# Hymba layer step on one core: first norm about a pivot, four x loads, and a different order of the first loads and products

## The chip, the cores and the metric

One NeuronCore of a Trainium2 chip runs the whole program in one launch. The metric is the device time in microseconds (us); lower is better. The kernel before took 1599.39 us as the median of three runs (1597.56 to 1601.09).

## What is computed

The reference is one layer of a hybrid recurrent transformer, for 256 prompt tokens and 8 x 4 sample tokens (288 tokens, 2048 features, float32). Only its beginning matters here:

```
mod = jax.nn.silu(c) @ w_ada + b_ada
sh1, sc1, g1, sh2, sc2, g2 = jnp.split(mod[:, None, :], 6, axis=-1)
h = layer_norm(x) * (1 + sc1) + sh1
z = (h @ w_in).astype(f32)
```

`layer_norm` takes mean and variance over the 2048 features of each token. After `z` come two recurrent mixers, an output projection, a second norm, a convolutional feed-forward part and a third norm. The rest of the program is the same text in both kernels.

## The kernel before

**Layout.** Features lie on the 128 partitions, tokens on the free axis: x is 16 tiles `xs[k]` of 128x288. A sum over features is a matmul by a matrix of ones: `colsum` adds a tile into one of four groups of 32 rows of a PSUM bank, and `total` copies that bank on ACT and multiplies it by ones again, so that every partition holds the sum.

**Products.** Weights come in granules of 128x1024 float32 (512 KB): `load_to` issues the load into a `raw` buffer on the SP queue, `high_to` casts it to float32r on ACT (`whi`), `low_to` subtracts on DVE (`wlo`). An activation tile is split the same way (`split`). `products` issues, per 128x128 block, three matmuls: whi by the high part, whi by the low part, wlo by the high part. `granule` keeps a few granules ahead. `raw` and `wlo` share seven buffers (NR), `whi` has four (NH).

**adaLN.** `mod` is made in steps of one 512 KB load (`araw`, NA = 7 buffers) and a group of small float32 matmuls each (`ada_step`). UNITS_ADA says which columns a unit of steps gives: ADA_K = (2, 2, 2, 2, 4, 4) means that the first unit gives shift and scale for two tiles of x, after eight steps. When a unit is done, `ada_finish` transposes the sums on DVE, adds the bias (`pks`), and puts `hidden(k)` on a list of background work; `tick` advances that list. `hidden` makes tile k of h.

**The start** (function `start`). SP issues ct, 16 loads of x, seven adaLN loads, two constants (`cs`, `pks`), and then what the steps and granules ask for. PE sums the 16 tiles; DVE scales to the mean `mu`; then each tile is centred (two in three on DVE, one in three on POOL), squared (ACT or DVE) and summed; `rstd_of` makes 1/sqrt(var) with Ln and Exp on ACT and three DVE operations. Then w_in is multiplied in five groups of k-tiles, KG = (2, 2, 4, 4, 4), for the first 28 (NSPLIT) column tiles: group 0 takes seven granules of four column tiles each, so it can begin when two tiles of h are there. Partial sums are copied out of PSUM by ACT in group 0 and added by DVE in later groups (`partial`). After every granule `credit` grows, and when it reaches four, four adaLN steps follow.

**What sets the order.** The schedule is the order in which the program text is written, engine by engine; each engine works its queue in order, and SP issues DMAs in order, waiting at each for its buffer to be free.

## Time and profile before

| | us |
|---|---|
| median of three runs | 1599.39 |
| the profiled execution | 1595.16 |
| its span, first to last instruction | 1593.4 |
| PE busy | 1552.8 (97%) |
| DVE busy | 1029.1 (65%) |
| ACT busy | 697.0 (44%) |
| POOL busy | 278.1 (17%) |

The profiled execution is 1.8 us longer than its span and 4.2 us shorter than the median. A busy share is an average over the span; the rows further below take stretches of it. PE is TensorE's matmuls, PEld its weight loads, DVE is VectorE, ACT ScalarE, POOL GpSimd, and SPq the queue on which SyncE issues DMAs. A float32 matmul leaves two records in the trace, a float32r one a single record.

### The profile page before, as it was taken

The numbers are of one execution on the slowest core, as the hardware profiler recorded it, in microseconds if no ns is written. First come the engines' busy times: TensorE is split into PE (matmuls) and PEld (weight loads), VectorE is DVE, ScalarE is ACT, GpSimd is POOL, SyncE is SP. The second block draws the span as 40 slices with busy tenths as digits, with TensorE's granted clock in tenths as the row PEclk, the third lists the DMA queues.
The fourth block names the chain that finished last, engine by engine and source line by source line (L and its number), as shares of the span: only waits on it lengthen the run. The fifth ranks groups of instructions, "written<-read, shape, count | busy, mean of one in ns | idle before, by whom it ended". The sixth has DMA issues, their size and how long they took to land.

```text
span 1593.4 us, 31779 instructions
## 1 busy us (share of the span) xinstructions
PE 1552.8 (97%) x12607; PEld 1454.4 (91%) x12607; DVE 1029.1 (65%) x2074; ACT 697.0 (44%) x1224; POOL 278.1 (17%) x434
## 2 busy tenths in 40 slices
PE   6999999999999989998999999999999999999998
PEld 3999989788898878886999999999999999999997
DVE  4566667887888778778855554555555555555555
ACT  3522335556656555335644333334343334343343
POOL 1000011444354343225311100011110001111000
PEclk9999999999999999998999999999999999999999
DMA  9898855778868778783544555555555555554552
GB/s 338 325 344 318 313 197 156 279 255 296 305 227 314 266 270 313 258 308 105 169 160 164 168 162 163 169 168 163 168 164 158 163 178 162 169 164 164 167 153 72
DMA packets 99269, 340.79 MB, mean 214 GB/s; under 512 B 11433, under 2 KB 18097, under 8 KB 98097
## 3 DMA queue, kind: packets, MB, share of 16 engines
q1 hardware_dynamic: 96624, 328.55, 60.1%
q0 software_dynamic: 2496, 10.22, 1.6%
q8 instruction: 99, 1.62, 0.4%
q14 instruction: 50, 0.40, 0.1%
HBM read 326.51 MB, written 12.21 MB: 213 GB/s over the span
## 4 chain that ended last, share of the span: by engine, by line
PE 84%; DVE 9%; ACT 3%; DMA 2%; issue 1%; SPq 0%; POOL 0%; ACTq 0%; DVEq 0%
PE mm L169 69%; PE sd L169 11%; DVE t L156 4%; PE ad L169 3%; ACT t L166 1%; DVE wlo L156 1%; DVE t L159 1%; DVE t L163 1%; ACT whi L229 1%; DMA raw<-w_in_b 1%; DVE c L159 1%; DMA t<-xt 1%; DMA raw<-w_out_b 0%; DMA pks<-pk 0%; ACT t L189 0%
## 5 line engine op out<-in xcount | busy, mean ns | idle before, releaser
L169 PE MATMUL mm<-t,whi 128*128 128x288 f32 (+1 forms) x4624 | 937.7, 298 | 16.9 <-ACT whi L229 9.2
L169 PEld LDWEIGHTS mm<-t,whi 128*128 128x128 f32 (+1 forms) x4624 | 741.4, 188 | 31.1 <-ACT whi L229 10.5
L169 PE MATMUL mm<-t,wlo 128*128 128x288 f32 x2312 | 683.4, 296 | 5.0 <-DVE wlo L156 5.0
L229 ACT CAST whi<-raw 128x1024 fp32r<-128x1024 f32 (+2 forms) x413 | 423.1, 1027 | 449.8 <-PE mm L169 226.0
L156 DVE TENSOR_TENSOR wlo<-raw,whi 128x1024 fp32r<-128x1024 f32 (+2 forms) x413 | 501.6, 1216 | 22.3 <-ACT whi L229 17.4
L169 PEld LDWEIGHTS mm<-t,wlo 128*128 128x128 f32 x2312 | 434.9, 188 | 6.8 <-DVE wlo L156 6.8
L169 PE MATMUL mm<-ff,whi 128*128 128x288 f32 x1376 | 276.1, 296 | 0.0
L169 PEld LDWEIGHTS mm<-ff,whi 128*128 128x128 f32 x1376 | 220.8, 188 | 2.5 <-issue 1.9
L166 ACT ACTIVATE t<-t 128x288 f32<-128x288 f32 (+4 forms) x329 | 126.2, 397 | 191.8 <-DVE t L156 137.6
L169 PE MATMUL mm<-ff,wlo 128*128 128x288 f32 x688 | 203.1, 295 | 0.0
L156 POOL TENSOR_TENSOR t<-t,t 128x288 f32<-128x288 f32 (+3 forms) x141 | 125.1, 896 | 183.5 <-ACT t L166 102.0
L159 DVE SCALAR_TENSOR_TENSOR t<-mm,mod,t 128x256 f32<-128x256 f32 x96 | 46.3, 482 | 149.2 <-PE mm L169 141.0
L169 PEld LDWEIGHTS mm<-ff,wlo 128*128 128x128 f32 x688 | 129.1, 188 | 0.0
L156 DVE TENSOR_TENSOR t<-t,t 128x288 f32<-128x288 f32 (+5 forms) x230 | 103.8, 473 | 24.8 <-ACT t L189 20.6
L1509 POOL COPY convo<-ext 128x2 f32<-128x2 f32 x43 | 8.0, 185 | 630.1 <-ACT ext L1503 630.1
L1504 DVE COPY ext<-mm 128x32 f32<-128x32 f32 x42 | 8.1, 192 | 141.1 <-ACT ext L1503 140.5
L169 PE MATMUL sd<-t,whi 128*128 128x288 f32 x464 | 95.5, 298 | 0.0
L169 PE MATMUL ad<-araw,csp 128*32 128x256 f32 (+1 forms) x1312 | 75.8, 362 | 0.8 <-DMA araw<-w_ada 0.8
L169 PEld LDWEIGHTS sd<-t,whi 128*128 128x128 f32 x464 | 75.9, 192 | 0.0
L156 DVE TENSOR_TENSOR t<-cv,mm 128x256 f32<-128x256 f32 x80 | 20.7, 300 | 78.9 <-PE mm L169 78.9
L169 PE MATMUL sd<-t,wlo 128*128 128x288 f32 x232 | 69.2, 298 | 0.0
L156 DVE TENSOR_TENSOR t<-t,mm 128x288 f32<-128x288 f32 x70 | 31.4, 450 | 52.6 <-PE mm L169 52.4
(253 smaller groups left out, 1171.0 us busy)
## 6 DMA issues: line engine op xcount, KB each, us to landing
araw<-w_ada SPq DMA_DIRECT2D x180, 512.0 KB, 5.6
raw<-w_up_b SPq DMA_DIRECT2D x160, 512.0 KB, 3.6
raw<-w_in_a SPq DMA_DIRECT2D x56, 512.0 KB, 6.7
raw<-w_in_b SPq DMA_DIRECT2D x56, 512.0 KB, 6.8
raw<-w_down SPq DMA_DIRECT2D x48, 512.0 KB, 3.5
raw<-w_down SPq DMA_DIRECT2D x32, 384.0 KB, 3.1
raw<-w_out_a SPq DMA_DIRECT2D x16, 512.0 KB, 6.5
raw<-w_out_b SPq DMA_DIRECT2D x16, 512.0 KB, 6.2
```

The source lines that it names most:

```text
L156: (eng or self.nc.vector).tensor_tensor(out=out, in0=a, in1=b, op=op)
L159: self.nc.vector.scalar_tensor_tensor(out=out, in0=a, scalar=s, in1=b, op0=op0, op1=op1)
L163: (eng or self.nc.vector).tensor_scalar(out=out, in0=a, scalar1=s1, scalar2=s2, op0=op0, **kw)
L166: self.nc.scalar.activation(out, a, f, **kw)
L169: self.nc.tensor.matmul(out, lhsT, rhs, start=start, stop=stop, **kw)
L229: self.nc.scalar.copy(hi[:, :w], raw[:, :w])
L1504: nc.vector.tensor_copy(se[:, :, 2:6], self.smp(pa))
L1509: nc.gpsimd.tensor_copy(co[:, j, 0:2], ext[:, TP:TP + 2])
```

## The change

All of it lies before the mixers, in about the first eighth of the program.

1. x comes in four loads of four tiles into one buffer of a pool of its own (`xin`), in place of 16 loads of one tile.
2. The norm is taken about a pivot: the mean of the first four tiles alone (`piv`). All 16 tiles have piv subtracted on DVE and are squared on ACT; one pass sums both x - piv (`s1`) and its square (`s2`). Mean offset `d` = s1/D, variance = s2/D - d*d + EPS. No tile is centred on POOL any more.
3. `normal(k)` subtracts d and multiplies by 1/std, for two tiles right away and for tile done + 2 after each granule; `hidden` loses its multiplication.
4. ADA_K begins with (1, 1, ...): the first unit gives one tile after four steps, the second the next tile after four more.
5. The order of the first loads on SP is written out, with the number of adaLN loads limited by `ad_limit` (8, 12, 15) and no longer by the number of steps done.
6. Six adaLN steps, in place of two, stand between the norm and the first granule, and the first weight cast stands after the fourth of them; five matmuls whose result nobody reads (`warm`) follow.
7. The first granule goes through `by_pass`: for all four column tiles first whi by tile 0's parts, then whi by tile 1's parts, and wlo at the very end.

The diff, cut at the places marked:

```diff
-ADA_K = (2, 2, 2, 2, 4, 4)
+ADA_K = (1, 1, 2, 2, 2, 4, 4)
...
-            if not ahead and s >= (self.ad_n if s < AD0 else max(self.ad_n, AD0 + NPRE)) + NA:
+            if s >= AD0 + NPRE and s >= max(self.ad_n, AD0 + NPRE) + NA:
                 break
...
-        xs = self.xs = [self.t288() for _ in range(KT)]
-        for k in range(KT):
-            nc.sync.dma_start(xs[k], i["xt"][:, k, :])
-        self.ada_load(NA)
+        xt = xin.tile([P, KT, T], F32, name="x")
+        for k in range(0, KT, 4):
+            nc.sync.dma_start(xt[:, k:k + 4, :], i["xt"][:, k:k + 4, :])
+        xs = self.xs = [xt[:, k, :] for k in range(KT)]
         a, b = CC["cap"][0], PK["b_ada"][1]
+        self.ad_limit = 8
+        self.ada_load(8)
+        nc.sync.dma_start(self.pks[:, :b], i["pk"][:, :b])
+        self.load_to(2)
+        self.ad_limit = 12
+        self.ada_load(12)
+        self.load_to(4)
+        self.ad_limit = 15
+        self.ada_load(15)
         nc.sync.dma_start(self.cs[:, :a], i["cst"][:, :a])
-        nc.sync.dma_start(self.pks[:, :b], i["pk"][:, :b])
...
-        sm = self.ps(T)
-        for k in range(KT):
-            self.colsum(sm, xs[k], k, KT)
-        mu = self.t288()
-        self.tsc(mu, self.total(sm), 1.0 / (32 * D), None, ALU.mult)
-        self.ada_step()
-        self.ada_step()
-        sq = self.ps(T)
-        for k in range(KT):
-            self.tt(xs[k], xs[k], mu, ALU.subtract, eng=nc.gpsimd if k % 3 == 2 else None)
-            s = self.t288()
-            if k % 4 == 3:
-                self.tt(s, xs[k], xs[k], ALU.mult)
-            else:
+        pv = self.ps(T)
+        for k in range(4):
+            self.colsum(pv, xs[k], k, 4)
+        piv = self.t288()
+        nc.scalar.mul(piv, self.total(pv), 1.0 / (32 * 4 * P))
+        s1, s2 = self.ps(T), self.ps(T)
+        for c in range(0, KT, 4):
+            sq = []
+            for k in range(c, c + 4):
+                self.tt(xs[k], xs[k], piv, ALU.subtract)
+                s = self.t288()
                 self.act(s, xs[k], AF.Square)
-            self.colsum(sq, s, k, KT)
-            if k % 4 == 1:
+                sq.append(s)
+            for k in range(c, c + 4):
+                self.colsum(s1, xs[k], k, KT)
+            for k in range(c, c + 4):
+                self.colsum(s2, sq[k - c], k, KT)
+            if c >= 8:
                 self.ada_step()
         var = self.t288()
-        self.tsc(var, self.total(sq), 1.0 / (32 * D), EPS, ALU.mult, ALU.add)
+        d = self.d = self.t288()
+        self.tsc(d, self.total(s1), 1.0 / (32 * D), None, ALU.mult)
+        self.tt(var, d, d, ALU.mult)
+        self.tsc(var, var, -EPS, None, ALU.add)
+        t2 = self.total(s2)
+        self.stt(var, t2, 1.0 / (32 * D), var, ALU.mult, ALU.subtract)
         self.rx = self.rstd_of(var)
+        for k in range(2):
+            self.normal(k)
...
-        self.load_to(2)
-        for _ in range(2):
+        for n in range(6):
+            self.ada_step()
             self.tick()
-            self.ada_step()
+            if n == 3:
+                self.tick()
+                self.high_to(1)
+        self.ad_limit = AD0
+        warm = self.ps(T)
+        for n in range(5):
+            self.mm(warm, self.ones, xs[KT - 1 - n], n == 0, n == 4)
...
+                sums = [self.ps(T, "sd" if j % 2 else "mm") for j in range(nj)] if done == 0 else None
+                if sums:
+                    self.by_pass(sums, hl, ks)
...
+                if done + 2 < KT:
+                    self.normal(done + 2)
...
+    def normal(self, k):
+        x = self.xs[k]
+        self.tt(x, x, self.d, ALU.subtract)
+        self.tt(x, x, self.rx, ALU.mult)
+
     def hidden(self, k):
...
-        self.tt(x, x, self.rx, ALU.mult)
```

**How the change moves the work.** In the rows below a name's number only tells one buffer of a kind from another.

The SP queue from the first load on, before: x tile by tile, seven adaLN loads, the constants, five more adaLN loads, then the first two weight granules (`raw`).

```order
L439 DMA t_78<-ct 128x144
L442 DMA t_80<-xt 128x288
...
L306 DMA araw_124<-w_ada 128x1024
L445 DMA cs<-cst 128x168
L446 DMA pks<-pk 128x96
L306 DMA araw_168<-w_ada 128x1024
...
L220 DMA raw_324<-w_in_a 128x1024
L220 DMA raw_326<-w_in_a 128x1024
L306 DMA araw_328<-w_ada 128x1024
L306 DMA araw_338<-w_ada 128x1024
L220 DMA raw_378<-w_in_a 128x1024
```

The same queue, changed:

```order
L441 DMA t_81<-ct 128x144
L444 DMA x<-xt 128x1152 x4
L306 DMA araw_88<-w_ada 128x1024
...
L306 DMA araw_102<-w_ada 128x1024
L449 DMA pks<-pk 128x96
L220 DMA raw_105<-w_in_a 128x1024
L220 DMA raw_107<-w_in_a 128x1024
L306 DMA araw_109<-w_ada 128x1024
...
L306 DMA araw_115<-w_ada 128x1024
L220 DMA raw_117<-w_in_a 128x1024
```

The first granule is now the ninth 512 KB load and no longer the thirteenth; the third granule (raw_117, raw_378 before) is the fifteenth and no longer the seventeenth, and `cs` goes behind all of these.

PE at the first granule, before: per column tile all six products, wlo from the third on (t_362 and t_363 are the parts of tile 0 of h, t_366 and t_367 those of tile 1).

```order
L169 MATMUL ad_159<-araw_168,csp 32x128 x8
L169 MATMUL mm_386<-t_362,whi_370 128x288
L169 MATMUL mm_386<-t_363,whi_370 128x288
L169 MATMUL mm_386<-t_362,wlo_372 128x288
L169 MATMUL mm_386<-t_366,whi_370 128x288
L169 MATMUL mm_386<-t_367,whi_370 128x288
L169 MATMUL mm_386<-t_366,wlo_372 128x288
L169 MATMUL sd_393<-t_362,whi_370 128x288
```

The same place, changed (t_388 and t_389 are tile 0, t_440 and t_441 tile 1):

```order
L169 MATMUL sd_351<-araw_102,csp 32x64 x16
L169 MATMUL sd_430<-x,ones 128x288 x5
L169 MATMUL mm_454<-t_388,whi_392 128x288
L169 MATMUL mm_454<-t_389,whi_392 128x288
L169 MATMUL sd_455<-t_388,whi_392 128x288
...
L169 MATMUL mm_454<-t_440,whi_392 128x288
L169 MATMUL mm_454<-t_441,whi_392 128x288
...
L169 MATMUL mm_454<-t_388,wlo_444 128x288
L169 MATMUL mm_454<-t_440,wlo_444 128x288
```

Eight products now need neither wlo nor tile 1, and eight more need no wlo; an adaLN step is 16 matmuls of 64 columns in the first two units, and eight of 128 before.

DVE from the third granule's low part on, before: low parts alone, and `hidden` with its multiplication (t_80 there is x).

```order
L156 TENSOR_TENSOR t_80<-t_80,t_289 128x288
L163 TENSOR_SCALAR t_352<-t_80,mod 128x256
...
L156 TENSOR_TENSOR wlo_372<-raw_324,whi_370 128x1024
L156 TENSOR_TENSOR wlo_376<-raw_326,whi_374 128x1024
L156 TENSOR_TENSOR wlo_417<-raw_378,whi_380 128x1024
L156 TENSOR_TENSOR wlo_496<-raw_382,whi_419 128x1024
```

DVE there, changed (t_263 is d, t_276 is 1/std):

```order
L156 TENSOR_TENSOR wlo_444<-raw_105,whi_392 128x1024
L156 TENSOR_TENSOR wlo_448<-raw_107,whi_446 128x1024
L156 TENSOR_TENSOR x<-x,t_263 128x288
L156 TENSOR_TENSOR x<-x,t_276 128x288
L156 TENSOR_TENSOR wlo_487<-raw_117,whi_450 128x1024
L156 TENSOR_TENSOR x<-x,t_263 128x288
L156 TENSOR_TENSOR x<-x,t_276 128x288
L156 TENSOR_TENSOR wlo_566<-raw_119,whi_489 128x1024
```

From the third granule on, the two operations of `normal` stand ahead of each granule's low part.

## Rows read from the trace of the kernel before

**Rows 1.** The page: busy time of each engine over the span.
```profile
PE 1552.8 (97%) x12607; PEld 1454.4 (91%) x12607; DVE 1029.1 (65%) x2074; ACT 697.0 (44%) x1224; POOL 278.1 (17%) x434
```

**Rows 2.** The two longest sums of PE's waits, 33 to 215 us: total, times, longest.
```profile
PE mm L169 <- ACT whi L229: 6.2, 1, 6.2
PE mm L169 <- DVE wlo L156: 2.3, 4, 1.5
```

**Rows 3.** Timeline to the first square: start, length, what, idle time before it and releaser.
```profile
3.84 7.93 PE L169 MATMUL sd<-t,ones 128*32 128x288 f32 x28 [3.84 <-DMA t<-xt]
...
12.69 0.14 PEld L169 LDWEIGHTS sd<-t,ones 128*32 128x32 f32 x2 [0.49 <-DMA t<-xt]
13.40 0.40 ACT L395 COPY t<-sd 128x288 f32<-128x288 f32 x1 [8.97 <-PE sd L169]
...
13.85 0.75 PE L169 MATMUL sd<-t,ones 128*128 128x288 f32 x2 [0.49 <-ACT t L395]
...
15.14 2.40 DVE L156 TENSOR_TENSOR t<-t,t 128x288 f32<-128x288 f32 x3
```

**Rows 4.** Timeline of DVE, ACT and PE from the last squares to the first products.
```profile
22.32 1.19 DVE L156 TENSOR_TENSOR t<-t,t 128x288 f32<-128x288 f32 x3
22.81 1.14 ACT L166 ACTIVATE t<-t 128x288 f32<-128x288 f32 x3 [0.29 <-DVE t L156]
26.29 1.08 PE L169 MATMUL ad<-araw,csp 128*32 128x128 f32 x32
26.40 0.46 DVE L163 TENSOR_SCALAR t<-sd 128x288 f32<-128x288 f32 x1 [2.40 <-PE sd L169]
26.89 0.92 ACT L166 ACTIVATE t<-t 128x288 f32<-128x288 f32 x2 [1.34 <-DVE t L163]
28.33 0.95 DVE L159 SCALAR_TENSOR_TENSOR t<-t,t 128x288 f32<-128x288 f32 x2
29.20 0.31 DVE L345 STREAM_TRANSPOSE adsb<-ad 128x128 f32<-128x128 f32 x1
30.98 0.43 ACT L189 CAST t<-t 128x288 fp32r<-128x288 f32 x1 [3.17 <-DVE t L156]
32.46 1.99 ACT L229 CAST whi<-raw 128x1024 fp32r<-128x1024 f32 x2
33.55 0.85 PE L169 MATMUL mm<-t,whi 128*128 128x288 f32 x2 [6.18 <-ACT whi L229]
```

**Rows 5.** The first two granules and the steps behind them; the third granule's cast.
```profile
34.81 0.61 PE L169 MATMUL mm<-t,wlo 128*128 128x288 f32 x1 [0.41 <-DVE wlo L156]
36.90 1.05 ACT L229 CAST whi<-raw 128x1024 fp32r<-128x1024 f32 x1 [2.46 <-DMA raw<-w_in_a]
42.96 1.95 PE L169 MATMUL sd<-araw,csp 128*32 128x128 f32 x64
44.84 0.53 PE L169 MATMUL mm<-t,whi 128*128 128x288 f32 x2
```

**Rows 6.** Stretches: us, busy time of PE, PEld, DVE, ACT, POOL, granted clock, DMA share, GB/s.
```profile
34.00:36.00 2.00, 1.59 (x7) 1.25 (x7) 1.89 (x2) 0.45 (x1) 0.00 (x0) 0.50 1.04 414
3.00:8.00 5.00, 4.16 (x12) 1.09 (x12) 0.62 (x2) 0.99 (x4) 0.00 (x0) 1.00 0.93 259
40.00:44.00 4.00, 4.00 (x63) 3.84 (x66) 1.57 (x2) 3.12 (x7) 0.00 (x0) 1.00 0.07 28
60.00:100.00 40.00, 39.77 (x509) 36.99 (x502) 29.04 (x65) 13.73 (x19) 0.00 (x0) 1.00 0.98 364
```

**Rows 7.** DMA packets from 3 to 12.5 us, and from 15 to 34 us.
```profile
DMA packets 2273, 2.64 MB, mean 278 GB/s; under 512 B 253, under 2 KB 2167, under 8 KB 2273
...
DMA packets 2374, 7.75 MB, mean 408 GB/s; under 512 B 391, under 2 KB 519, under 8 KB 2373
```

**Rows 8.** Tile vm: duration ns min/median/max, first and last start.
```profile
L169 PE MATMUL sd<-vm,stk x32: 390/400/507, 267.1 to 631.0; 96*128 96x512 f32 x32
L156 POOL TENSOR_TENSOR vm<-stk,cs x16: 1890/1894/2866, 251.2 to 620.0; 96x1024 fp32r<-96x1024 f32 x16
```

More of the change, by code (lines that the diff above doesn't have):

```diff
@@ L430, in run, with start @@
         self.ad_stop, self.ad_limit, self.ad_tag = AD0 - 4, AD0, "sd"
-        self.start()
+        with tc.tile_pool(name="xin", bufs=1) as xin:
+            self.start(xin)
         self.mixer()
         self.tail()
-    def start(self):
+    def start(self, xin):
         nc, i = self.nc, self.i
@@ L488, in start @@
                 hl = self.granule()
+                sums = [self.ps(T, "sd" if j % 2 else "mm") for j in range(nj)] if done == 0 else None
+                if sums:
+                    self.by_pass(sums, hl, ks)
                 for j in range(nj):
-                    ps = self.ps(T, "sd" if j % 2 else "mm")
-                    self.products(ps, hl, j * ks * P, self.h[k0:k0 + ks], True, True)
+                    if sums:
+                        ps = sums[j]
+                    else:
+                        ps = self.ps(T, "sd" if j % 2 else "mm")
+                        self.products(ps, hl, j * ks * P, self.h[k0:k0 + ks], True, True)
                     self.tick()
                     self.bg.append(self.partial(self.z[nj * p + j], ps, g == 0))
+                if done + 2 < KT:
+                    self.normal(done + 2)
                 self.credit += 2 if done < 14 or done % 3 == 0 else 1
@@ L499, in start, with by_pass @@
             self.tick()
+    def by_pass(self, sums, hl, ks):
+        hi, lo = hl
+        for q, (xh, xl) in enumerate(self.h[:ks]):
+            for j, ps in enumerate(sums):
+                c = slice((j * ks + q) * P, (j * ks + q + 1) * P)
+                self.mm(ps, hi[:, c], xh, q == 0, False)
+                self.mm(ps, hi[:, c], xl, False, False)
+        for j, ps in enumerate(sums):
+            for q, (xh, xl) in enumerate(self.h[:ks]):
+                c = slice((j * ks + q) * P, (j * ks + q + 1) * P)
+                self.mm(ps, lo[:, c], xh, False, q == ks - 1)
     def partial(self, a, ps, first):
```

## The prediction

> **What bounds the kernel now.** Start with the page: PE is busy for 97% of the span [rows 1]. That is an average, so look next at PE's waits, by stretch. From 33 to 215 us PE waits 6.2 us once, for the cast of its first weights, and 2.3 us in four pieces for low parts [rows 2]; between 60 and 100 us it is busy for 39.77 of 40 us [rows 6]. So from its first product on PE is the bound, and a time saved ahead of that product, or in the half-clock stretch behind it, moves the rest of the program forward, as long as PE's data keep up. The timeline says what comes ahead. The first product starts at 33.55 us [rows 4]; before it lie the arrival of x (to 12.7 us), the mean (first tile centred at 15.14) [rows 3], centring and squares (to 23.95), variance and 1/std (to 29.2), two tiles of h and the first cast [rows 4]. [...] PE's last work before was an adaLN step that ended at 27.37, 6.18 us before the first product [rows 4].
>
> All differences below are against the profiled execution (span 1593.4 us, 1.8 us around it, 1595.16 in all); the median is 4.2 us above that, and I add those at the end.
>
> **x.** Up to 12.5 us nearly all packets are under 2 KB (2167 of 2273, 1.2 KB each on average) and 278 GB/s flow; from 15 us on, with 512 KB loads, it is 408 GB/s at 3.3 KB [rows 7], and in the former stretch the engines are just as busy (share 0.93 at 259 GB/s) [rows 6]. So the size of the packets costs, and four tiles in one load give rows four times as long. I take 408 GB/s. Bounds: 278 and 408. The first tile was there at 3.84 us [rows 3]; three more (0.44 MB, 1.1 us) complete the first load at 4.9 us, and the other 12 tiles (1.77 MB, 4.3 us) end at 9.25, 3.4 us earlier than now. [...]
>
> **The norm.** The pivot needs only the first load. Four column sums (1.2 us: the last one of now takes 0.7 from its weight load at 12.69 to the copy at 13.40, and four of them overlap in part), copy 0.40, total 0.75 [rows 3], the scaling on ACT 0.40 as that copy: 4.9 + 2.75 + 0.15 of handovers = 7.85 us, where now it is 15.14. Centring is 16 DVE operations of 0.40 (1.19 for three) with the square 0.38 behind each on ACT [rows 4]: 14.25, last square 14.7, its sum 15.1. Now this takes until 23.95, because POOL shares it and three DVE operations cost 2.40 us [rows 3]. Then the price of the single pass: an adaLN step stands on PE ahead of the totals. A step is 16 records now, and two in a row take 1.08 us [rows 4], 0.54 each; in the change it is 32 records of half the columns, between 0.54 (columns count) and 1.08 us (records count). [...] Total 0.75, d, its square, -EPS and the variance on DVE 4 x 0.47 = 1.9, Ln and Exp 0.92, three DVE operations 1.45 [rows 4]: 21.05. Two `normal` 4 x 0.43 = 1.7: 22.75. From the transpose at 29.20 to the cast at 30.98 it is 1.78 with one multiplication of 0.47 [rows 4], without it 1.3: 24.05. Cast of tile 0 0.43, of the weights 1.0: **first product at 25.6 us**, 7.95 earlier.
>
> Are its weights there? Load pieces of 512 KB take 1.285 us each at 408 GB/s. The first granule is the ninth: 9.25 + 9 x 1.285 + 0.1 for pks = 20.9 us. The eighth adaLN load must wait until step 0 frees a buffer, at about 13.5 us; at that time seven pieces are queued to 18.2, so SP's wait leaves no hole. adaLN step 7 needs the eighth piece (19.6) and ends by 20.5 to 22 us; the five idle matmuls (2 records each, 0.5 us per pair) end at 23 to 24.5, ahead of the first product. They cost nothing, since PE has nothing else then.
>
> **The first two granules.** Two granules take PE 6.35 us at full clock; now they took from 33.55 to the steps at 42.96 [rows 4, 5], 9.4 us: 0.41 waiting for the low part [rows 5] and about 2.6 at half clock [rows 6]. In the change PE idles 1 to 2.5 us before the first product, against the 6.18 us after which the clock was low, so I take full clock: -2.6. `by_pass` takes the low part's wait away, but a new wait comes: eight products of tile 0 are done in 1.05 us, and tile 1 comes later. DVE makes the low part of tile 0, transposes, and makes tile 1 (1.8 us after the first product's start with its cast), then the first low part (1.15): granule 0 ends 4.1 us after its start, 29.7. Granule 1 needs a PSUM bank, the bank a copy on ACT, and that copy stands in ACT's queue behind the cast of the third granule, which is piece 15: 9.25 + 19.3 + 0.1 = 28.65, cast 1.05, copy 0.40: **30.1**. So this wait, not the low part, starts granule 1. It ends at 33.3, the four steps behind (1.95) at 35.3. In the trace of before that point is 44.84 [rows 5]: **-9.5 us**.
>
> **Behind it.** PE's order is the same from here, but for which PSUM bank a unit of adaLN uses. Do loads keep up? At 35.3 about 20 pieces are there, one fewer than at 44.84 now, for now DMA lay idle at 40 to 44 us (share 0.07) with full buffers [rows 6]; PE asks six pieces in 8.45 us, DMA can give them in 7.7. I charge 0.5 us for pauses in that stream (0 to 3). DVE gets `normal` 14 times behind granules, 0.9 us each (12.6), and loses 14 multiplications of 0.45 in `hidden` (6.3). At 60 to 100 us it is busy 29.04 of 40 [rows 6]; with nine `normal` more and four multiplications less, 35.3 of 40: it fits, tightly where a unit's two tiles of `hidden` fall together with partial sums. I charge 0.5 us (0 to 3). POOL's set-up instruction for its first two-input operation moves from before 15 us to ahead of the first `vm` at 251.2; that result lies ready at 254.1, and PE takes the first at 267.1 [rows 8]. No row shows how long the set-up takes; up to the cover of 13 us it costs nothing, and I take nothing.
>
> **Sum:** -9.5 + 0.5 + 0.5 = -8.5. Profile 1586.7; median 1599.4 - 8.5 = **1591 us**. Either bound of the uncertain terms gives 1586 at best (pauses and DVE nothing, granule 1 at 29.7, 1.8 us of scatter between runs); its own range is 1587 to 1595.
>
> **Rivals.**
> *Half clock again* (0.13). PE's work in the norm is short sums with gaps, and if the clock is low when products begin, the 2.6 us are lost again, and up to 2 more while sums run slowly: 1594 to 1596. For it: low clock after 27.37 [rows 4, 6]. Against: less idle time, the five idle matmuls.
> *x no faster* (0.07). x ends at 12.7 as now; the third granule comes 3.4 us later (at 32.1; now its cast waits for it until 36.90 [rows 5]), granule 1 at 33.5: 1594. [...] Against: packets and shares [rows 6, 7].
> *DMA is the bound from there* (0.10). At 60 to 100 us DMA is busy 0.98 at 364 GB/s [rows 6], and PE asks 372. If that is its limit, PE, started early, runs into its loads, and what stays is what the loads gained, 0 to 3.4 us: 1596 to 1599, no change or little. Against: no wait of PE for a load there [rows 2], and 408 GB/s earlier [rows 7].
> *DVE decides* (0.05), on the other side. `normal` stands ahead of each low part. If DVE has no room per granule, each of 14 granules waits 0.9 us: +12.6 against -9.5, 1602.5. It decides once DVE's work per granule passes PE's: four partial sums, one low part and one `normal`, 4 x 0.45 + 1.2 + 0.9 = 3.9 us, against 4.2 of PE. That is near, but partial sums on DVE begin only with the eighth granule, so the likely price is 3 us, 1594.
> *Forecast* (0.62); something unseen, 0.03.
>
> **The numbers.** A measurement can tell about 0.2%, 3.2 us. Faster by more: most of the forecast, half clock and slow x, a third of the DMA case: 0.82. Within: 0.13. Slower: 0.05. The range, 1586 to 1597, reaches into the DMA case.
>
> **What would show it.** Last column sum of the first load near 6 us, first centring near 8, first product near 26 us; granted clock 1.00 from there; PE's wait before granule 1 ended by ACT behind a DMA; the first four full steps done near 35 us; the waits of PE from there to 205 us still near zero. A half-clock stretch after 25 us, PE waiting for `raw` or `araw` at 40 to 100, or for wlo in the second group of granules would prove one of the rivals.

## The result, and the profile after

| | before | after |
|---|---|---|
| median, four runs of each on one chip (us) | 1600.24 | 1587.06 |
| lowest to highest | 1597.56 to 1601.87 | 1584.66 to 1588.47 |
| ratio, 95% interval | | 0.9927 [0.9914, 0.9941] |
| profiled execution | 1595.16 | 1587.27 |
| its span | 1593.4 | 1585.4 |

The changed kernel is 0.7% faster, 9 to 14 us by the interval of the ratio (the medians alone differ by 13.2). The two profiled executions differ by 8.0 us only in their spans, since that of before was one of the quicker ones. The time lies inside the forecast range of 1586 to 1597 us, but near its lower end, 4 us below the forecast of 1591. The inner points of the forecast did not hold: the first batch of four steps came 6.7 us earlier and not 9.5, and the rest was won behind it. First the page; PE's row answers to [rows 1].

```profile
PE 1547.0 (98%) x12755; PEld 1456.8 (92%) x12755; DVE 1033.2 (65%) x2096; ACT 699.1 (44%) x1230; POOL 274.0 (17%) x429
```

The timeline of the changed kernel (start, length, engine, line, what; in brackets the idle time before it and its releaser), from the first load of x to the first batch of steps; it answers to [rows 3 to 5]:

```profile
5.66 1.19 PE L169 MATMUL sd<-x,ones 128*32 128x288 f32 x8 [5.66 <-DMA x<-xt]
7.41 1.33 PE L169 MATMUL sd<-t,ones 128*128 128x288 f32 x2 [0.56 <-ACT t L395]
9.22 1.93 DVE L156 TENSOR_TENSOR x<-x,t 128x288 f32<-128x288 f32 x5 [4.42 <-ACT t L469]
...
14.68 0.69 PE L169 MATMUL sd<-t,ones 128*32 128x288 f32 x1
...
15.70 0.41 PE L169 MATMUL sd<-t,ones 128*32 128x288 f32 x1
...
17.35 0.80 PE L169 MATMUL ad<-araw,csp 128*32 128x64 f32 x32
...
20.17 1.97 PE L169 MATMUL sd<-araw,csp 128*32 128x64 f32 x128
...
27.56 0.53 PE L169 MATMUL mm<-t,whi 128*128 128x288 f32 x2 [2.80 <-ACT whi L229]
31.50 1.05 ACT L229 CAST whi<-raw 128x1024 fp32r<-128x1024 f32 x1 [1.81 <-DMA raw<-w_in_a]
32.46 0.39 ACT L548 COPY t<-mm 128x288 f32<-128x288 f32 x1
32.90 0.53 PE L169 MATMUL mm<-t,whi 128*128 128x288 f32 x2
...
36.27 1.95 PE L169 MATMUL ad<-araw,csp 128*32 128x128 f32 x64
```

The pivot is ready before the last x, and the first centring comes at 9.22 where it was at 15.14. The first product starts 6.0 us earlier. The second granule needs the copy of a PSUM bank, which stands behind the cast of the third granule, which waits for its load: the row at 31.50, where before it was 36.90. In this trace PE does not stand idle for the copy. It is done at 32.85, the products of the first granule, slow from 29.3 us on, end about then too, and the second granule starts at 32.90; which of the two sets that start, the runs with no and with ten idle matmuls tell. Two matmuls of one form, 0.69 us at 14.68 and 0.41 at 15.70, show that TensorE ran slowly until about 15.6 us (the column of the granted clock shows 1.00 there all the same). The stretches (us; busy time and count of PE, PEld, DVE, ACT, POOL; granted clock; DMA share; GB/s) show where it was slow again:

```profile
29.30:32.70 3.40, 3.40 (x14) 3.40 (x15) 3.15 (x5) 1.59 (x3) 0.00 (x0) 0.50 1.02 406
60.00:100.00 40.00, 40.00 (x481) 37.15 (x483) 35.15 (x79) 12.07 (x14) 0.00 (x0) 1.00 0.96 360
206.80:210.10 3.30, 3.18 (x12) 2.90 (x12) 0.06 (x1) 0.00 (x0) 0.00 (x0) 0.50 0.52 159
```

From 60 to 100 us PE is busy for all 40.00 us, though DVE is at 35.15 (39.77 and 29.04 before) [rows 6]. From 33 to 203 us no wait of PE is left at all. DMA's packets from 3 to 10 us, against [rows 7]:

```profile
DMA packets 684, 2.77 MB, mean 395 GB/s; under 512 B 70, under 2 KB 70, under 8 KB 684
```

Where the lead stands along the program (before minus after): first product 6.0 us (33.55 to 27.56), first batch 6.7 (42.96 to 36.27), the batch at 98.55 us 7.2, at 156.47 us 7.6, the first `vm` 6.4 (251.24 to 244.89), the end 8.0. It grows by 0.9 where the kernel before lost time at three batches: they came 8.78, 8.77 and 12.01 us behind the ones ahead of them, in the changed kernel 8.46, 8.47 and 11.58. A fourth, at 187.61 us in the kernel before, brings the lead to 8.0. It shrinks again at 204.78 to 210.81, where PE waits 1.68, 0.55 and 0.64 us (before 1.53, 0.55 and 0.64) and the half-clock stretch above follows; the trace of before has none there.

### The profile page after: what moved, and what is told of

It is laid out like the page before. It is cut to its first block, busy times and chain, and to the rows that moved or that the text cites. A ratio compares the mean times of both kernels' runs of the same rounds, so it can differ in the third digit from the quotient of the medians.

```text
span 1585.4 us, 32088 instructions
## 1 busy us (share of the span) xinstructions
PE 1547.0 (98%) x12755; PEld 1456.8 (92%) x12755; DVE 1033.2 (65%) x2096; ACT 699.1 (44%) x1230; POOL 274.0 (17%) x429
## 3 DMA queue, kind: packets, MB, share of 16 engines
q8 instruction: 101, 1.65, 0.4%
## 4 chain that ended last, share of the span: by engine, by line
PE 86%; DVE 8%; ACT 3%; DMA 2%; issue 1%; SPq 0%; POOL 0%; ACTq 0%; DVEq 0%
PE mm L169 70%; PE sd L169 12%; PE ad L169 4%; DVE t L156 3%; DVE wlo L156 2%; ACT t L166 1%; DVE t L159 1%; ACT whi L229 1%; DVE c L159 1%; DMA raw<-w_in_b 1%; DMA raw<-w_out_b 0%; DMA pks<-pk 0%; DVE t L163 0%; DMA x<-xt 0%; ACT t L189 0%
## 5 line engine op out<-in xcount | busy, mean ns | idle before, releaser
L156 DVE TENSOR_TENSOR wlo<-raw,whi 128x1024 fp32r<-128x1024 f32 (+2 forms) x413 | 501.6, 1215 | 15.4 <-ACT whi L229 10.5
L166 ACT ACTIVATE t<-t 128x288 f32<-128x288 f32 (+4 forms) x317 | 121.5, 395 | 187.2 <-DVE t L156 130.4
L156 POOL TENSOR_TENSOR t<-t,t 128x288 f32<-128x288 f32 (+3 forms) x136 | 120.8, 896 | 168.6 <-ACT t L166 101.0
L156 DVE TENSOR_TENSOR t<-t,t 128x288 f32<-128x288 f32 (+4 forms) x203 | 89.8, 464 | 25.3 <-ACT t L189 21.2
L169 PE MATMUL ad<-araw,csp 128*32 128x256 f32 (+2 forms) x1312 | 68.4, 345 | 0.0
```

Source lines behind the costliest of these rows:

```text
L156: (eng or self.nc.vector).tensor_tensor(out=out, in0=a, in1=b, op=op)
L166: self.nc.scalar.activation(out, a, f, **kw)
L169: self.nc.tensor.matmul(out, lhsT, rhs, start=start, stop=stop, **kw)
```

## The experiments

Theory: the lead comes from four things in a chain, the quick loads of x, the pivot, an earlier third granule, and VectorE work taken out of `hidden`; what the idle matmuls and the clock do around 30 us does not reach the second granule. Rivals stand with each run. Each ratio is to the kernel before, run in the same rounds. The changed kernel was not run again beside its variants; its ratio is that of the result above. The table is read with this in mind: kernels whose order of work hardly differs can lie 3 us apart in the median (1587.06, 1584.38 and 1583.96 us with five, no and ten idle matmuls), and half-clock stretches behind 200 us stand in some traces and not in others, so places in the trace tell more than the medians. They too carry some chance: in the kernels that leave the sums as they are, TensorE's clock rose at 12.5 to 13.2 us in four traces (ten idle, units of two, old order, `normal` inside `hidden`) and at 15.3 to 15.6 in three (changed, no idle, no by-pass). Two of the early ones, ten idle and `normal` inside `hidden`, have the first batch 1.0 and 1.2 us sooner by that.

| kernel | ratio [95%] | first product | first batch | first vm |
|---|---|---|---|---|
| changed kernel | 0.9927 [0.9914, 0.9941] | 27.56 | 36.27 | 244.89 |
| no idle matmuls | 0.9904 [0.9883, 0.9925] | 27.45 | 36.28 | 242.68 |
| ten idle matmuls | 0.9904 [0.9884, 0.9923] | 27.45 | 35.25 | 241.62 |
| early idle matmuls | 0.9931 [0.9911, 0.9951] | 33.00 | 39.65 | 245.84 |
| x in 16 loads | 0.9963 [0.9949, 0.9977] | 29.02 | 41.85 | 250.28 |
| adaLN units of two | 0.9947 [0.9935, 0.9959] | 25.24 | 36.49 | 243.12 |
| units of two, early idle | 0.9935 [0.9917, 0.9953] | 26.05 | 34.73 | 243.25 |
| the same, copies first | 0.9934 [0.9922, 0.9946] | 28.36 | 35.02 | 241.22 |
| no pivot | 0.9966 [0.9955, 0.9977] | 28.07 | 38.63 | 245.38 |
| all of it, few idle | 0.9938 [0.9924, 0.9951] | 25.87 | 32.84 | 245.68 |
| old order of loads | 0.9940 [0.9925, 0.9954] | 29.17 | 37.93 | 245.06 |
| normal inside hidden | 0.9995 [0.9980, 1.0011] | 25.35 | 35.06 | 255.80 |
| no by-pass | 0.9935 [0.9920, 0.9949] | 27.33 | 38.95 | 245.45 |

### x in 16 loads

```
-        for k in range(0, KT, 4):
-            nc.sync.dma_start(xt[:, k:k + 4, :], i["xt"][:, k:k + 4, :])
+        for k in range(KT):
+            nc.sync.dma_start(xt[:, k, :], i["xt"][:, k, :])
```

> The changed kernel with x in 16 loads of a tile in place of four loads of four tiles. Theory: x ends near 12.7 us as in the kernel before, every load behind it lands about 2.9 us later, the third granule's at 34.4, and the first batch of four steps is at 39.1 in place of 36.27 us: 2.9 us more in all; the pivot itself moves little, as four small loads are there by about 5.6 us. Rival: sixteen loads are as fast as four, and nothing moves (the gain is all in the order of the work).

x is complete at 12.41 us in place of 9.82, and everything queued behind it comes later. Timelines of ACT and PE:

```profile
34.60 1.04 ACT L229 CAST whi<-raw 128x1024 fp32r<-128x1024 f32 x1 [5.14 <-DMA raw<-w_in_a]
35.99 0.85 PE L169 MATMUL mm<-t,whi 128*128 128x288 f32 x2 [3.41 <-ACT t L548]
41.85 1.96 PE L169 MATMUL ad<-araw,csp 128*32 128x128 f32 x64
```

The third granule's cast is 3.1 us later than in the changed kernel, and the second granule with it, as the theory had it. The batch is 5.6 us later and not 2.9: behind the wait of 3.41 us the clock was granted at 0.50 from 34.7 to 41.5. In the end 0.36% are lost, half of the change's gain, and the intervals are apart. From 4 us to the end of x the DMA engines of this run and of the changed kernel (the columns as in the stretches above) were busy like this:

```profile
4.00:12.00 8.00, 6.52 (x39) 2.26 (x39) 3.77 (x12) 4.09 (x12) 0.00 (x0) 1.00 0.92 274
...
4.00:9.80 5.80, 2.58 (x11) 0.80 (x12) 0.93 (x4) 1.22 (x4) 0.00 (x0) 1.00 1.02 417
```

With rows of 1152 bytes the engines were nearly as busy (share 0.92 against 1.02) and moved a third less (274 against 417 GB/s), so here the size of the rows counts, and not only the number of loads.

### No pivot

```
-        for k in range(4):
-            self.colsum(pv, xs[k], k, 4)
+        for k in range(KT):
+            self.colsum(pv, xs[k], k, KT)
...
-            for k in range(c, c + 4):
-                self.colsum(s1, xs[k], k, KT)
```

> The changed kernel without the pivot: the mean over all 16 tiles first, then centring and squares, one multiplication in the normalisation; loads, order of loads, by-pass and idle matmuls stay. Theory: the mean waits for the last load of x (9.82), so the first centring comes near 12.8 us (9.22), and the squares' last sum near 21 us, the first product 2 to 3 us later, near 30 us; the first granule ends near 34 us, past the third granule's load (31.5), so about 1 to 2 us of it reach the first batch (37.5 to 38.5 us) and the end. Rival: all comes from the earlier loads, since the second granule waits for the third's load in any case: batch at 36.3 us and no difference.

Timelines of DVE, SP's queue and PE:

```profile
13.16 3.04 DVE L156 TENSOR_TENSOR x<-x,t 128x288 f32<-128x288 f32 x8 [8.39 <-ACT t L469]
19.36 0.33 SPq L306 DMA_DIRECT2D araw<-w_ada  x1
28.07 0.53 PE L169 MATMUL mm<-t,whi 128*128 128x288 f32 x2 [1.03 <-ACT whi L229]
35.26 0.53 PE L169 MATMUL mm<-t,whi 128*128 128x288 f32 x2 [3.01 <-ACT t L541]
```

The batch moved as expected, by 2.4 us, but by another road. The first product comes only 0.5 us later than with the pivot. What is late is the eighth adaLN load: its buffer comes free when step 0 has run, and without the pivot it is issued at 19.36 us (16.8 with it), so that every load behind it waits, the third granule's too, and the second granule stands 3.01 us. That load lands 2.4 us later (33.84 us, 31.48 with the pivot), and the batch follows it. So the pivot's worth on the path is that it lets SP go on. The medians differ by 5.3 us (0.39%, intervals apart). The traces show 2.4 us of that, which stay to the end (spans of 1587.8 and 1585.4 us); where the rest comes from is not shown.

### The idle matmuls: none, ten

```
         warm = self.ps(T)
-        for n in range(5):
-            self.mm(warm, self.ones, xs[KT - 1 - n], n == 0, n == 4)
+        for n in range(10):
+            self.mm(warm, self.ones, xs[KT - 1 - n], n == 0, n == 9)
```

In the other kernel all four lines are gone.

> The changed kernel without its five idle matmuls (22.07 to 24.76 us there). Theory: the point that decides is the start of the second granule at 32.90 us, which waits for the landing of raw for the third granule (31.48), not for the clock; the idle matmuls only shorten the time in which TensorE has no work, and without them the half-clock stretch becomes two in a row (6.8 us, about 29.3 to 36.1, as in the kernel before), of which the second lies in the second granule: the first batch of four steps behind it moves from 36.27 to about 38 us and the kernel takes 1.5 to 1.7 us more. Rival: the clock drops once, as it does with them, and nothing moves: 36.3 us and no difference.

> The changed kernel with ten idle matmuls in place of five, so that TensorE is busy until about 27.4 us, up to the first product (27.56). Theory: the half-clock stretch 29.29 to 32.70 goes, the first granule ends earlier, but the second starts at 32.9 all the same, since its PSUM copy stands behind the cast of the third granule (landing 31.48): the first batch of four steps stays at 36.3 and the time within 0.3 us. Rival: the clock is what holds the first two granules, and 1.7 us are gained: batch at 34.6.

Without them, PE's timeline and the stretch:

```profile
27.45 0.85 PE L169 MATMUL mm<-t,whi 128*128 128x288 f32 x2 [5.42 <-ACT whi L229]
36.28 1.95 PE L169 MATMUL ad<-araw,csp 128*32 128x128 f32 x64
...
25.80:32.50 6.70, 5.05 (x21) 5.05 (x22) 5.31 (x13) 3.82 (x6) 0.00 (x0) 0.50 1.02 410
```

With ten of them, ACT's and PE's timelines and the stretch:

```profile
30.49 1.05 ACT L229 CAST whi<-raw 128x1024 fp32r<-128x1024 f32 x1 [1.77 <-DMA raw<-w_in_a]
31.88 0.53 PE L169 MATMUL mm<-t,whi 128*128 128x288 f32 x2 [0.89 <-ACT t L548]
35.25 1.96 PE L169 MATMUL ad<-araw,csp 128*32 128x128 f32 x64
...
24.00:36.00 12.00, 10.56 (x89) 9.18 (x91) 10.16 (x24) 6.96 (x13) 0.00 (x0) 1.00 1.02 401
```

The half-clock stretch doubles without them (25.7 to 32.5) and is gone with ten, and in neither run does that move the batch by more than 0.1 us. With none it lies wholly ahead of 32.9, the time at which the second granule may start; I had put its second half behind that, and so expected 1.5 us that did not come. With ten the first granule ends early and PE waits 0.89 us for the copy; the batch is 1.02 us earlier, but so is the third granule's cast (30.49 for 31.50), since the clock rose at 13.1 us in that run and step 0 freed its buffer sooner. The five idle matmuls are worth nothing that these runs show; the load of the third granule decides. It lands at 31.48, 31.42 and 30.46 us with five, none and ten, and the batch comes 4.79, 4.86 and 4.79 us behind it. The same 4.79 us lie between the two in four more traces: no pivot, old order, `normal` inside `hidden`, and units of two with early idle matmuls.

### Early idle matmuls, and adaLN units of two

```
+        first = self.ps(P)
+        for n in range(9):
+            self.mm(first, self.ones, self.ones, n == 0, n == 8)
         pv = self.ps(T)
...
-ADA_K = (1, 1, 2, 2, 2, 4, 4)
+ADA_K = (2, 2, 2, 2, 4, 4)
```

The first part (with two more such matmuls behind the pivot's sums, four behind its total, and ten late ones) is one kernel, the second another, and both together a third.

> Ten idle matmuls as in the kernel beside it, and 15 short matmuls on the ones: nine ahead of the first column sums (about 1.4 to 5.3 us), two while the pivot's sums are copied, four while x is centred, so that TensorE hardly pauses from the start. Theory: the granted clock reaches 1.00 by about 9 us in place of 15.63, the sums no longer lag behind the squares (last one near 16 us, now 17.3), the first product starts near 26.2 us (27.56), and step 0 runs earlier, so that the eighth adaLN load is issued about 1 us sooner, the hole in the loads gets smaller, and the third granule lands up to 1 us earlier: first batch near 35.3 us, 1 us less in all. Rival: DMA sets the third granule regardless, and the batch stays at 36.3 us.

> The changed kernel with the first adaLN units of two tiles each, as in the kernel before: the first eight adaLN steps hold the same data in 16 records in place of 32, so TensorE has 256 instructions fewer ahead of the first product. Theory: TensorE's instructions come in blocks of 16 KB (256 instructions; one block is in the trace about every 256 matmuls and weight loads), each fetched by the DMA engines behind the loads that are queued there; TensorE can be held when it runs through a block faster than the one after next comes. In the changed kernel it arrives just after the blocks, so nothing is won here by itself: first product within 0.7 us of 27.56, first batch of four steps at 35.3 to 36.5 us, set by the third granule's load; time within 1 us. Rival: the shorter first units are what brings tile 0 early, and the first product comes 1 us or more later, at 28.5 us.

> The kernel with 15 early idle matmuls and ten later ones, now with adaLN units of two tiles. In the same kernel with units of one tile TensorE stood for 2.06 us at 19.94 and for 4.31 us at 26.24 with nothing that the trace names, at its 449th and 705th instruction. Theory: there it waited for blocks of its own instructions (landing 18.5 and 24.9). With 256 instructions fewer, those instructions come later in the program, both waits go, the first product moves from 33.00 to 25 to 26 us and the first batch from 39.65 to 35.0 to 35.5 us, then set by the third granule's load. Rival: the waits are for adaLN loads (the eighth lands at 21.2 us) or for the idle matmuls' operands, and a wait of 4 us before the first product stays: batch near 39 us.

With the early matmuls the clock was high from 6.1 us, the sums were done by 16, and still the first product came 5.4 us later than in the changed kernel. PE's timeline (the row at 33.00 follows the ten late idle matmuls, 6.8 us, half of it at half clock):

```profile
16.96 0.91 PE L169 MATMUL ad<-araw,csp 128*32 128x64 f32 x49
19.94 0.37 PE L169 MATMUL ad<-araw,csp 128*32 128x64 f32 x12 [2.06 <-issue]
20.11 0.22 PE L169 MATMUL sd<-araw,csp 128*32 128x64 f32 x1
20.13 0.23 PE L169 MATMUL ad<-araw,csp 128*32 128x64 f32 x3
20.16 1.77 PE L169 MATMUL sd<-araw,csp 128*32 128x64 f32 x112
26.24 0.43 PE L169 MATMUL sd<-araw,csp 128*32 128x64 f32 x15 [4.31 <-issue]
33.00 0.65 PE L169 MATMUL mm<-t,whi 128*128 128x288 f32 x2
```

PE waits for "issue", that is, for nothing that the trace names. Between the two waits lie 12 + 1 + 3 + 112 = 128 matmuls and as many weight loads, 256 instructions. And among the data a packet of another queue passes at 17.3 to 18.6 us, and again at 23.6 to 25. The DMA view of the first stretch (queue, kind: packets, MB, share), and that queue over the whole run:

```profile
q1 hardware_dynamic: 138, 0.50, 97.7%
q8 instruction: 1, 0.02, 5.3%
...
q8 instruction: 101, 1.65, 0.4%
```

The 101 packets of this queue hold 1.65 MB, 16 KB each, and the run has 25,590 matmuls and weight loads, 253 to a packet. So I take them for TensorE's instructions; the trace does not say what a packet holds, but each of the two waits ends 1.3 to 1.4 us behind the landing of one (18.5 and 24.9). With units of two tiles, 256 instructions fewer ahead of the products, both waits are gone:

```profile
19.37 0.65 PE L169 MATMUL ad<-araw,csp 128*32 128x128 f32 x16 [0.39 <-DMA araw<-w_ada]
20.73 0.64 PE L169 MATMUL ad<-araw,csp 128*32 128x128 f32 x16 [0.71 <-DMA araw<-w_ada]
26.05 0.64 PE L169 MATMUL mm<-t,whi 128*128 128x288 f32 x2
31.36 0.54 PE L169 MATMUL mm<-t,whi 128*128 128x288 f32 x2 [1.77 <-ACT t L555]
34.73 1.95 PE L169 MATMUL sd<-araw,csp 128*32 128x128 f32 x64
```

That is the theory's result: batch at 34.73 for 39.65. Waits for "issue" at the same counts of instructions stand in four more kernels with units of one tile (0.56 and 0.55 us with ten idle matmuls, 0.58 with 16 loads, 1.17 with the old order, 1.09 with `normal` inside `hidden`); the changed kernel itself just gets by. Units of two alone bring the first product to 25.24, 2.3 us earlier, where I had expected next to nothing (the clock rose at 12.5 us in that run, and the steps have half the records; the runs don't part the two). But the second granule then waits 2.48 us for the copy, for the third granule's load lands at 30.16 us, 1.3 sooner than in the changed kernel and no more; a half-clock stretch (33.0 to 36.4) takes that back, and the batch stays at 36.49. So the theory is too narrow in one point: a half-clock stretch inside the second granule does reach the batch, here and with 16 loads of x.

### PSUM copies ahead of the third granule's cast

```
-        self.high_to(n + NH - 1)
+        self.high_to(n + NH - 1 - (n == 0))
...
+                if done == 1:
+                    self.tick()
                 hl = self.granule()
```

> As the kernel beside it, and the four PSUM copies of the first granule stand ahead of the cast of the third granule in ScalarE's queue, so that the second granule needs no load of the third. Theory: with full clock and no wait for instructions, the second granule starts as soon as the first is done (29 to 30 us) in place of 31.9, and the first batch comes 1.5 to 2.5 us earlier, at 33 to 33.7 us; the rest of the program follows if loads keep up. Rival: DMA is the bound from there, the third granule or the adaLN loads of the next batch hold TensorE by as much, and from 60 us on the program stands where the kernel beside it stands.

> The kernel with adaLN units of two tiles, early idle matmuls and PSUM copies ahead of the third granule's cast, but with three late idle matmuls in place of ten (there they ran at half clock until 28.4 us, four us past the time at which the first product's operands were ready), and two short idle matmuls behind each of the last six adaLN steps, where TensorE waited 0.7 us for each load. Theory: the first product starts at 24.5 to 25.5 us, the second granule follows the first without a wait, the first batch comes at 31.3 to 32.5 us (36.27 in the changed kernel), and as long as loads keep up the program stays 3.5 to 4.5 us ahead of it: 1583 against 1587. Rival: loads do not keep up; TensorE waits for raw or araw between 33 and 60 us, and from 60 us on the program is about 1.5 us ahead, as the kernels whose first batch came at 34.7 and 35.0 us.

In the former of these two the ten idle matmuls, from 22.08 on, took 6.65 us, about half of it at half clock. The operands of the first product were ready at about 24.7 and it started at 28.36, so the cover itself cost 3.7 us (1.5 of it by the clock, for with early idle matmuls and units of two the same ten took 5.12 us), and the batch came no earlier (35.02 for 34.73). The other kernel, with three idle matmuls, shows what the order of the copies is worth. Timelines of ACT and PE:

```profile
28.97 0.40 ACT L559 COPY t<-mm 128x288 f32<-128x288 f32 x1 [1.55 <-PE mm L169]
...
30.36 1.05 ACT L229 CAST whi<-raw 128x1024 fp32r<-128x1024 f32 x1
...
29.57 0.43 PE L169 MATMUL mm<-t,whi 128*128 128x288 f32 x2
32.84 1.95 PE L169 MATMUL sd<-araw,csp 128*32 128x128 f32 x64
```

The second granule (29.57) follows the first without a wait, ahead of the cast (30.36) behind which it stands in the changed kernel. The batch is 3.4 us ahead of the changed kernel's, 2.5 of that still at 154 us. And yet the run is no faster. At 203 us PE waits for a low part, 2.45 us here, and then the clock is low for 10 us:

```profile
PE mm L169 <- DVE wlo L156: 2.5, 1, 2.5
...
204.60:214.60 10.00, 8.81 (x36) 8.44 (x36) 3.92 (x7) 1.82 (x3) 0.00 (x0) 0.50 0.32 102
```

So the first half of the theory held (the second granule need not wait), and in this trace the gain was given back by that wait and the clock behind 200 us. That stretch is in the profiled run of this kernel; how often it comes in others of its runs was not seen. No kernel here is shown to beat the changed one; the two best medians (none, ten idle matmuls) have intervals that overlap its own.

### Old order of loads, no by-pass

```
-        self.ad_limit = 8
-        self.ada_load(8)
+        self.ada_load(NA)
...
-        self.load_to(2)
-        self.ad_limit = 12
-        self.ada_load(12)
-        self.load_to(4)
...
-            if s >= AD0 + NPRE and s >= max(self.ad_n, AD0 + NPRE) + NA:
+            if not ahead and s >= (self.ad_n if s < AD0 else max(self.ad_n, AD0 + NPRE)) + NA:
```

and, in another kernel,

```
-                sums = [self.ps(T, "sd" if j % 2 else "mm") for j in range(nj)] if done == 0 else None
+                sums = [self.ps(T, "sd" if j % 2 else "mm") for j in range(nj)] if done < 0 else None
```

> The changed kernel with the order of loads of the kernel before: seven adaLN loads, then the constants, then each further adaLN load when a step has run, and the first weight load behind the sixth step. x still comes in four loads. Theory: the first granule's weights come behind 13 adaLN loads, at about 28 us (23.07), the third granule's at about 34 (31.48), the first product near 29.5 us and the first batch near 39 us, 2.5 to 3 us later than 36.27. Rival: the order of loads is worth nothing, as the pivot and the quick arrival of x made the gain: batch at 36.3 us.

> The changed kernel with the first granule's products in the usual order, low part third. Theory: TensorE waits in the first granule until the first low part is done (about 30.3 us) after the first two products at 27.56, which is 2 us or more; the granule ends near 33.5 us, little later than the 32.9 at which the second granule could start anyway, and the batch comes at 36.8 to 37.2 us; up to 1.7 us more if the wait brings a half-clock stretch into the second granule. Rival: the order makes no difference, since the third granule's load sets the second granule's start: batch at 36.3 us.

With the old order PE waits 4.17 us for the first weights (first product 29.17) and the batch is 1.7 us later, as the third granule's load is (33.14 for 31.48). I had expected 2.5 to 3; the clock rose 2.4 us sooner in that run than in the changed kernel. Without the by-pass:

```profile
30.18 0.61 PE L169 MATMUL mm<-t,wlo 128*128 128x288 f32 x1 [2.32 <-DVE wlo L156]
38.95 1.95 PE L169 MATMUL ad<-araw,csp 128*32 128x128 f32 x64
```

The wait came as expected, with half clock from 28.9 to 35.7, and the batch is 2.7 us later. At the end of the traces 2.5 us (order) and 1.4 us (by-pass) remain; the medians lie 2.7 and 1.5 us above the changed kernel with intervals that overlap, so these two parts are seen in the traces only.

### Normal inside hidden

```
-        for k in range(2):
-            self.normal(k)
...
-                if done + 2 < KT:
-                    self.normal(done + 2)
...
         x = self.xs[k]
+        self.normal(k)
         hf = self.t288()
```

> The changed kernel with each tile's subtraction and multiplication at the head of hidden, none ahead of need. Theory: the first tile's h comes up to 0.9 us earlier, the first batch stays at 36.3 us (third granule's load), but in 60 to 190 us each unit of tiles asks 0.9 us more of VectorE per tile just when TensorE waits for it: waits of 0.9 to 1.4 us for low parts near 66 and 82 us, where the kernel before had 0.41 and 0.48 (with one multiplication there), and 2 to 3 us in all by 200 us. Rival: VectorE has room enough for both operations there, no waits appear, and normalising ahead of need is worth nothing.

This undoes the whole gain. PE's waits from 33 to 203 us, where the changed kernel has none:

```profile
PE mm L169 <- ACT t L189: 3.8, 3, 1.4
PE mm L169 <- DVE wlo L156: 1.1, 2, 0.5
PE mm L169 <- DVE t L156: 1.0, 1, 1.0
```

ACT's cast of the third granule:

```profile
30.29 1.04 ACT L229 CAST whi<-raw 128x1024 fp32r<-128x1024 f32 x1 [1.96 <-DMA raw<-w_in_a]
```

The first batch is 1.2 us earlier, but not because VectorE has less ahead of it: the clock rose at 13.1 us in that run, the eighth adaLN load was issued at 15.4 (16.8 in the changed kernel), and the third granule's load landed 1.2 us earlier. Then each new unit of tiles costs PE 1 to 2 us of waiting, four times, and half-clock stretches follow at 183.8 and from 214.5 to 224.7: the first `vm` is 10.9 us later. I expected 2 to 3 us; it was twice that in waits, and the clock on top. The medians of this run and of those with 16 loads and without the pivot lie 11.9, 7.1 and 5.3 us above the changed kernel's, together more than the whole gain: the parts depend on each other and do not add up. Two parts have no run of their own, the six adaLN steps ahead of the first granule and the place of the first weight cast.

## Why the prediction was right, point by point

**x.** Right in its rate: the four loads land 1.42 to 1.44 us apart, 412 GB/s. The start was 0.65 us late (5.53, not 4.9). Undoing the part cost 0.36%, so the rival of x no faster falls. While x came in, rows of 1152 bytes moved at 274 GB/s and rows of 4608 at 417.

**The norm.** The chain was right, the sizes too small: first centring 9.22 (7.85), last sum done at 17.7 (15.1), first product 27.56 (25.6). The step at fault took the totals and sums at full-clock durations. [Rows 3] gave 0.75 us for a total; it took 1.33 at 7.41, since TensorE was slow until 15.6. The chain from 15.1 to 21.05 holds 0.9 us for the adaLN step ahead of the totals, an estimate that no run shows: that step, at 17.35, took 0.80. Where four stood in a row, a step of 32 records took 0.5 us (1.97 for four), and so did one of 16 records of twice the columns (1.95), so columns count there and not records. Two additions of the prediction are also off, by amounts that change nothing: 4.9 + 2.75 + 0.15 is 7.8, and the terms up to the first product give 25.5.

**Loads.** "SP's wait leaves no hole" failed. Step 0 ran at 15.6, not 13.5, and the eighth adaLN load, issued at 16.8, landed 2.30 us behind the seventh, where a load takes 1.28. The first granule's weights were there at 23.07 (20.9), the third granule's at 31.48 (28.65).

**The first two granules.** The mechanism was right: the second granule starts behind copy, cast and the third granule's load (32.90; forecast 30.1, 2.8 late by the load). The sign that the prediction named for it, a wait of PE ended by ACT, is not in this trace, where slow products fill the time; it is in the run with ten idle matmuls (0.89 us). The size at this point was wrong by as much, -6.7 for -9.5. "I take full clock: -2.6" was wrong, for the clock fell from 29.29 to 32.70, but here free of cost: the runs with no idle matmuls and with ten show the batch following the load, not the clock. That was luck in part, as the slow products ended just when the copy was done.

**Behind it.** Here the two charges of +0.5 were of the wrong sign. Loads never held PE, and `normal` ahead of need did not crowd VectorE (35.15 of 40 us at 60 to 100, forecast 35.3), it took away waits. The lead grew from 6.7 to 7.6 us by 156 us, and the last experiment points at what stands behind it: with both operations inside `hidden`, where the kernel before had one, the first `vm` is 10.9 us later. The forecast of -8.5 against -8.0 in the traces is so the sum of a gain that was over-sized by 2.8 and others that were missed. That they nearly cancel is luck. POOL's set-up cost nothing, as forecast: its two records in the trace (MODIFY_POOL_CONFIG, 8 ns each) stand at 244.78 and 244.81, the first `vm` follows at 244.89 and takes 2.78 us, and PE first uses it at 260.6.

**Rivals.** Half clock again did come. Behind the first product it cost nothing; in the sums ahead of it, it is part of the 2 us by which the first product was late. DMA as the bound did not come. DVE decides was the real danger, with the mechanism of [rows 6] but at another place: not each granule behind a `normal`, but a unit's tiles in `hidden` when `normal` is not done ahead.

The gain is also more than the forecast, 11.7 us by the ratio (13.2 by the medians) against 8.4. Of this the traces cannot tell the cause: at 250 us the lead is 6.4, and from there on the two programs are the same; the kernel before has half-clock stretches of 13.6 us in all between 650 and 760 us, the changed one 6.8 between 580 and 750, which gives 3.4 us of work at half speed. Eight of the twelve variants have 13.7 us of it between 560 and 760 us, so nothing shows that the change is what spared it. Why the stretches come where they do was not tried.

## What to carry to other kernels

Find the wait that starts the second piece of work, not the first: here the variants moved the first product between 25 and 33 us, and in most of them the first batch followed the third granule's load, through a cast that stood ahead of a copy in one queue. A reduction that is made earlier can pay by the buffer that it frees for the next load. Work that an early finish piles onto another engine has to be spread ahead of need, or it takes the whole gain back.

## What the hardware showed that I had not expected

- Packets of the kind "instruction" pass on the DMA engines among the data, 16 KB each: 101 of them, 1.65 MB, in the run with early idle matmuls. There PE resumed at 19.94 and again at 26.24 us: 256 short instructions, done in 2 us, cost 6.3 while loads were queued; why a packet comes so late was not tried. With 256 instructions fewer ahead of the products both waits (2.06 and 4.31 us) were gone, so short matmuls ahead of full queues should be few.
- PE waits behind 200 us in all kernels, two or three times in a row, 1.75 to 3.64 us in all around 205. There is no half-clock stretch behind these waits in eight of the twelve variants, one of 3.4 us in two and in the changed kernel, and 10.2 us of it in two. The five kernels with a stretch waited 2.66 to 3.64 us and most of the others 1.75 to 2.23, but the old order (2.75) and the kernel before (2.72) have no stretch either. At the granted 0.50 a stretch of 3.4 us takes 1.7 us of TensorE's work. So gains of 2 us ahead of such a place can be lost in the median.
- Idle matmuls meant to hold the clock can themselves run at half clock in part (ten of them took 6.65 us in one run and 5.12 in another), and then delay the work that they were to speed.
